# Tracing the transposed a and the products N V inside the second half of a chunk inverse, in a two-layer RWKV-7 and differential-attention encoder

## The chip, the cores and the metric

The kernel runs on one core of one Trainium2 chip. The metric is the device time of one execution in microseconds (us). Three executions of the kernel before were timed; the median counts.

## The reference, cut to what matters

The model has two layers over 2048 rows of width 1024. Layer 0 is RWKV-7 time mixing in parallel with a small cross-attention; layer 1 is differential attention. Only layer 0 bears on this change. Per head it runs this recurrence over time:

```python
z = z + (token_shift(z) - z) * mu
r, k, v, wd, ad = split(z)
kk = k * k_k;  kk = kk * rsqrt(max(sum(kk * kk), 1e-12))
def step(state, inp):
    sa = einsum('bhvk,bhk->bhv', state, -kk_t)
    state = state * w_t + sa[..., None] * (kk_t * a_t) + v_t[..., None] * k_t
    y_t = einsum('bhvk,bhk->bhv', state, r_t)
    return state, y_t
```

z is the normalised input times a wide weight; the output y is normalised per head and gated before the output projection.

## The kernel before, in words

The kernel computes the recurrence in chunks of 64 rows. Inside a chunk the rank-one updates are a triangular system, so each chunk needs the inverse of a 64x64 unit triangular matrix and a few products with it; between chunks a 64x64 state per head is carried.

Layer 0 goes over two halves of 1024 rows; in each half over six pairs of heads; in each pair over two blocks of 512 rows. One pair and block is a `Step`, 24 in all. A step handles 8 chunks of two heads at once. Its parts are methods of `Step`, and the loop at the end of `layer_a` traces them in this order for i = 0, 1, ...: `p2` and `p3` of step i+1, `p4b` and `p5` of step i, `p3b` and `p4` of step i+1, then `filler(i + 2)`, which traces the gate of step i+1 and `p1` of step i+2.

- `p1` makes the projections. Each (`pj`, line 174) is 24 products of 128x512 that accumulate in one bank of PSUM: the gate `sil`, then `kx`, `rx` and `vx`. Line 295 (ACT) and lines 296 to 298 (DVE) mix a projection with its shifted self. From `kx` follow `kk` (line 357, DVE), its square `rn` (line 359, ACT) and the product `pss` (line 367, TensorE), which sums the squares. `cum` and `Pt` (lines 344 to 355) are the decays, from the small products `lr`.
- `p2` makes the products `pg` and their masked copy `Gm`, and the transposes `bkp` and `pvt`.
- `p3` inverts 16x16 diagonal blocks by 15 levels of two small DVE operations (`itmp` and `Ti`, lines 453 and 455) and writes them out in two layouts, `T16` (lines 460 and 462) and `TT16` (lines 464 and 466).
- `p3b` puts the blocks together to `TT`: two rounds of products `inv` (line 481, with the copy `E1` between them), then `Ta` (line 487), the products `invz`, their copy (line 496), the products `invr`, and the copy into `TT` (line 502).
- `p4` makes the transposed a (`atp`, line 520, 8 products against the identity) and N V (`nvp`, line 528, 16 products), copies both, negated, into the two tiles `X` (lines 522 and 530, ACT), multiplies by the inverse (`txp`, line 539), copies the results to `Wn` and `UV`, and makes `mrp` and the first part of `ch` (line 563).
- `p4b` carries the state through 8 chunks: for each a product `ch` (line 574) and a scaled copy to `S` on ACT (line 575), which the next `ch` reads; and the outputs `yp` (lines 583 and 588).
- `p5` copies them to `ys` (line 590), takes statistics (line 597), subtracts and scales (lines 607 and 608), transposes (`py`, line 611) and stores.

The order on each engine isn't written out by hand. The order in which the code is traced gives each instruction its priority; a scheduler then places instructions of neighbouring steps between each other on every engine at build time. On the chip each engine runs its list. Small tiles of `p3` to `p4` share the tag "iv" of 4 buffers (`M_`, `E1`, `X1`, `X2`, `T16`, `TT16`, `X`, `Wn`), and small PSUM tiles share the tag "gm" of 3 banks.

Of the kernel before, what the change touches and what calls it, by code (L numbers as in the profile page):

```python
# [10 lines left out]
AF = mybir.ActivationFunctionType  # L11
# [4 lines left out]
P = 128  # L16
# [8 lines left out]
C = 64  # L25
TB = 512
NC = TB // C
NJ = NC // 2
# [31 lines left out]
def hybrid_kernel(ctx, tc, S, HALF, x, mem, pv, cv, dist, postn, w_out, w_mkv, a_w, w2, a2, w_kv, b_w, out):  # L60
# [3 lines left out]
    mm = nc.tensor.matmul  # L64
    V = nc.vector
    A = nc.scalar
# [18 lines left out]
    def cc(name, w):  # L85
        return cvt[:, CV[name]:CV[name] + w]

    ident = cc("ident", 128)
# [120 lines left out]
    def layer_a(ph):  # L209
# [31 lines left out]
        def T(shape, name, bufs=1, tag=None, dt=F32):  # L241
            return pa.tile(shape, dt, name=name, tag=tag or name, bufs=bufs)
# [7 lines left out]
        def I(shape, name, dt=F32):  # L250
            return pa.tile(shape, dt, name=name, tag="iv", bufs=4)

        def PS(shape, name, tag="gm", bufs=3):
            if tag == "pj":
                return ppj.tile(shape, F32, name=name, tag="pj", bufs=3)
            return pps.tile(shape, F32, name=name, tag=tag, bufs=bufs)
# [69 lines left out]
        class Step:  # L326
# [141 lines left out]
                self.t3 = Nv, E1, T16, TT16  # L468

            def p3b(self):  # L470
                Nv, E1, T16, TT16 = self.t3

                TT = T([P, NJ, 2, 64], "TT", 1)

                def blk16(lt, rt_):
                    pb = PS([P, NJ, 2, 64], "inv")
                    for j in range(NJ):
                        for hh in range(2):
                            for q in range(2):
                                rows = slice(q * 64, q * 64 + 64)  # L480
                                mm(pb[rows, j, hh, :], lhsT=lt[rows, j, hh, :], rhs=rt_[rows, j, hh, :], start=True, stop=True)
                    return pb
                A.activation(E1, blk16(E1, T16), AF.Copy)
                V.tensor_tensor(out=TT, in0=blk16(E1, TT16), in1=TT16, op=ALU.add)

                Ta = T([P, NJ, 2, 32], "Ta", 1)
                V.transpose(out=Ta.rearrange("p j h t -> p (j h) t"), in_=TT.rearrange("p j h t -> p (j h) t")[:, :, 0:32])
                pz = PS([P, NJ, 2, 32], "invz")
                pr = PS([P, NJ, 2, 32], "invr")
                qa, qb = ([slice(q * 64 + o, q * 64 + o + 32) for q in range(2)] for o in (0, 32))  # L490
                for j in range(NJ):
                    for hh in range(2):
                        for q in range(2):
                            mm(pz[qb[q], j, hh, :], lhsT=Nv[q][0:32, j, hh, 32:64], rhs=Ta[qa[q], j, hh, :], start=True, stop=True)
                for q in range(2):
                    A.activation(Ta[qb[q]], pz[qb[q]], AF.Copy)
                for j in range(NJ):
                    for hh in range(2):
                        for q in range(2):
                            mm(pr[qa[q], j, hh, :], lhsT=Ta[qb[q], j, hh, :], rhs=TT[qb[q], j, hh, 32:64], start=True, stop=True)  # L500
                for q in range(2):
                    V.tensor_copy(out=TT[qa[q], :, :, 32:64], in_=pr[qa[q]])
                self.TT = TT
# [4 lines left out]
            def p4(self):  # L508


                AR, Gm, BKT, UV, TT = self.AR, self.Gm, self.BKT, self.UV, self.TT
                ar = (slice(64, 128), slice(0, 64))
                rr = (slice(0, 64), slice(64, 128))
                hcs = (slice(0, 64), slice(64, 128))

                X = [I([P, 2, 2, P], "X") for g in range(2)]
                pt = PS([P, NJ, P], "atp")
                for j in range(NJ):
                    for e in range(2):
                        mm(pt[ar[e], j, :], lhsT=AR[:, 2 * j + e, ar[e]], rhs=ident, start=True, stop=True)  # L520
                for g in range(2):
                    A.activation(X[g][:, :, :, 0:C], pt.rearrange("p j (h k) -> p j h k", h=2)[:, g * 2:g * 2 + 2], AF.Copy, scale=-1.0)
                pn = PS([P, NJ, 2, C], "nvp")
                for j in range(NJ):
                    for hh in range(2):
                        for e in range(2):
                            c = 2 * j + e
                            mm(pn[ar[e], j, hh, :], lhsT=Gm[rr[e], e, j, hh, ar[e]], rhs=UV[rr[e], c, hcs[hh]], start=True, stop=True)
                for g in range(2):
                    A.activation(X[g][:, :, :, C:P], pn[:, g * 2:g * 2 + 2], AF.Copy, scale=-1.0)  # L530
                Wn = I([P, NJ, 2, C], "Wn")
                UV4 = UV.rearrange("p (j e) (h v) -> p j e h v", e=2, h=2)
                for g in range(2):
                    js = slice(g * 2, g * 2 + 2)
                    px = PS([P, 2, 2, P], "txp")
                    for j in (g * 2, g * 2 + 1):
                        for hh in range(2):
                            for e in range(2):
                                mm(px[ar[e], j % 2, hh, :], lhsT=TT[ar[e], j, hh, :], rhs=X[g][ar[e], j % 2, hh, :], start=True, stop=True)
                    A.activation(Wn[:, js], px[:, :, :, 0:C], AF.Copy)  # L540
                    for e in range(2):
                        A.activation(UV4[ar[e], js, e], px[ar[e], :, :, C:P], AF.Copy)

                MT = self.MTs
                MT4 = MT.rearrange("p (j e) k -> p j e k", e=2)
                RT = T([P, NC, C], "RT", 1)
                AR4 = AR.rearrange("p (j e) t -> p j e t", e=2)
                pmr = [PS([P, NJ, P], "mrp") for e in range(2)]
                for j in range(NJ):
                    for hh in range(2):  # L550
                        for e in range(2):
                            mm(pmr[e][hcs[hh], j, 0:C], lhsT=Wn[ar[e], j, hh, :], rhs=BKT[ar[e], 2 * j + e, hcs[hh]], start=True, stop=True)
                            mm(pmr[e][hcs[hh], j, C:P], lhsT=Wn[ar[e], j, hh, :], rhs=Gm[ar[e], e, j, hh, rr[e]], start=True, stop=True)
                for e in range(2):
                    for hh in range(2):
                        hs = hcs[hh]
                        V.tensor_tensor(out=MT4[hs, :, e, hs], in0=pmr[e][hs, :, 0:C], in1=ident[hs, None, hs].broadcast_to([C, NJ, C]), op=ALU.add)
                    V.tensor_tensor(out=RT.rearrange("p (j e) t -> p j e t", e=2)[:, :, e], in0=pmr[e][:, :, C:P], in1=AR4[:, :, e, rr[e]], op=ALU.add)

                ch = pps.tile([P, NC, C], F32, name="ch", tag="ch", bufs=2)  # L560
                for c in range(NC):
                    for hh in range(2):
                        mm(ch[hcs[hh], c, :], lhsT=BKT[:, c, hcs[hh]], rhs=UV[:, c, hcs[hh]], start=c == 0, stop=False, skip_group_check=True)
                self.MT, self.RT, self.ch = MT, RT, ch
# [228 lines left out]
    class MemAttn:  # L793
# [30 lines left out]
        def T(self, shape, name, dt=F32, bufs=None):  # L824
            return self.pool.tile(shape, dt, name=name, tag=name, bufs=bufs or 1)

        def tile(self, t, yh, yl, PS):
# [7 lines left out]
            for m in range(2):  # L835
# [4 lines left out]
                mx = T([P, 4], "mmx")  # L840
                V.tensor_reduce(out=mx[:, 0:2], in_=ps, op=ALU.max, axis=AX.X)  # L841
                V.tensor_scalar(out=mx[:, 0:2], in0=mx[:, 0:2], scalar1=-SCALE, scalar2=None, op0=ALU.mult)
# [290 lines left out]
    def layer_b_attn(ep, prefetch):  # L1133
        with ExitStack() as st:
# [38 lines left out]
            def scores(u):  # L1173
# [3 lines left out]
                for qt in range(2):  # L1177
# [7 lines left out]
                    for c in range(2):  # L1185
# [16 lines left out]
                        E.append(e)  # L1202
                    V.tensor_reduce(out=nm[:, 0:2], in_=mx[:, :, 0:nkb], op=ALU.min, axis=AX.X)  # L1203
                    for c in range(2):
# [77 lines left out]
    with pool_(name="w_next", bufs=1) as rp:  # L1282
# [17 lines left out]
        for i in range(KT):  # L1300
            hf, k = i // 4, slice(i % 4 * 2, i % 4 * 2 + 2)
# [81 lines left out]
```

## Time and profile before

| | |
|---|---|
| median of three runs | 3139.35 us (3136.95 to 3140.87) |
| the profiled execution's own time | 3131.17 us |
| its span, first to last instruction | 3129.4 us |
| TensorE (PE) busy in the span | 2944.0 us, 94% |
| VectorE (DVE) / ScalarE (ACT) / GpSimd (POOL) busy | 57% / 48% / 27% |
| layer 0 | up to about 1420 us of the span |

PE, PEld, DVE, ACT, POOL are the engines (PEld is the load of TensorE's stationary operand). A matmul of 4-byte numbers can stand as two records in the trace, so record counts there can be twice those of the program. "PEclk" is TensorE's granted clock as a share of full speed: 1.00 is 2.4 GHz, 0.50 is 1.2 GHz.

### The profile page before, as it was taken

What the parts mean: (1) busy time and instruction counts of PE and PEld (TensorE: products, weight loads), DVE (VectorE), ACT (ScalarE), POOL (GpSimd) and SP (SyncE); (2) the same over time, 40 slices, a digit from 0 to 9 for tenths busy, and PEclk for the clock granted to TensorE, in tenths of its full rate; (3) what the DMA queues carried; (4) which work ended last, traced back from release to release, by engine and by line L of the source; (5) the groups of instructions that cost most, each with busy time, mean ns of one, the idle gap of its engine ahead of it and who ended that gap; (6) DMA issues with size and microseconds to landing.
All of it is one profiled execution on the core that took longest, in us unless ns stands there. A gap on an engine that the chain in (4) does not pass through costs nothing. (4 is left out here: it accounts for less than half of the span.)

```text
span 3129.4 us, 57336 instructions
## 1 busy us (share of the span) xinstructions
PE 2944.0 (94%) x22378; PEld 2390.8 (76%) x22378; DVE 1794.5 (57%) x4728; ACT 1504.3 (48%) x3310; POOL 840.2 (27%) x881
## 2 busy tenths in 40 slices
PE   6889999997899999998999999999999999998999
PEld 4767777776677777777777798888887888786777
DVE  6566767655676767673565311101118988887554
ACT  5545454545545454444454513213226777776443
POOL 3143423432243433431001212302212222323000
PEclk8899999998899999999999999999999999999999
DMA  3211000122011000115544533433355455543453
GB/s 119 78 33 37 28 24 23 39 61 84 26 30 37 28 24 24 38 45 142 147 135 127 147 86 91 118 86 92 102 164 123 101 113 115 122 85 103 129 153 116
DMA packets 262895, 264.13 MB, mean 84 GB/s; under 512 B 16736, under 2 KB 203232, under 8 KB 262496
## 3 DMA queue, kind: packets, MB, share of 16 engines
q1 hardware_dynamic: 234464, 193.87, 21.4%
q0 software_dynamic: 28160, 66.60, 10.4%
q8 instruction: 176, 2.88, 0.4%
q14 instruction: 95, 0.78, 0.1%
HBM read 179.14 MB, written 81.26 MB: 83 GB/s over the span
## 5 line engine op out<-in xcount | busy, mean ns | idle before, releaser
L174 PE MATMUL pj<-hhi,wh 128*128 128x512 f32 x928 | 389.6, 420 | 9.2 <-ACT sil L301 2.6
L174 PE MATMUL pj<-hhi,wl 128*128 128x512 f32 x928 | 375.3, 404 | 0.6 <-POOL wl L123 0.6
L174 PE MATMUL pj<-hlo,wh 128*128 128x512 f32 x928 | 368.5, 397 | 0.0
L123 POOL TENSOR_TENSOR wl<-wraw,wh 128x512 fp32r<-128x512 f32 x160 | 210.5, 1325 | 497.2 <-ACT wh L122 477.3
L1200 DVE CUSTOM_DVE_ANT_0 E<-s,dist 128x512 f32<-128x512 f32 (+1 forms) x480 | 276.1, 605 | 35.0 <-PE s L1198 28.9
L174 PE MATMUL pj<-bh,wh 128*128 128x512 f32 x672 | 262.8, 391 | 0.0
L174 PE MATMUL pj<-bh,wl 128*128 128x512 f32 x672 | 262.6, 391 | 0.0
L174 PE MATMUL pj<-bl,wh 128*128 128x512 f32 x672 | 262.5, 391 | 0.0
L1205 ACT ACTIVATE E<-E,nm 128x1920 f32<-128x1920 f32 (+7 forms) x192 | 229.4, 1199 | 59.1 <-DVE nm L1203 58.6
L174 PEld LDWEIGHTS pj<-hhi,wh 128*128 128x128 f32 x928 | 175.8, 189 | 63.7 <-ACT sil L301 8.9
L1238 PE MATMUL o<-th,vs 128*128 128x256 f32 (+1 forms) x864 | 211.0, 376 | 2.3 <-ACT th L1231 0.9
L1197 PE MATMUL s<-ks,qd 128*128 128x512 f32 (+1 forms) x480 | 205.6, 432 | 2.2 <-DVE mx L1200 1.2
L174 PEld LDWEIGHTS pj<-hhi,wl 128*128 128x128 f32 x928 | 175.4, 189 | 40.7 <-POOL wl L123 1.5
L174 PEld LDWEIGHTS pj<-hlo,wh 128*128 128x128 f32 x928 | 176.2, 190 | 38.8 <-issue 5.5
L122 ACT ACTIVATE wh<-wraw 128x512 fp32r<-128x512 f32 x160 | 100.3, 627 | 217.0 <-PE pj L174 139.4
L1238 PEld LDWEIGHTS o<-th,vs 128*128 128x128 f32 x864 | 153.9, 189 | 38.3 <-ACT th L1231 18.8
L1198 PE MATMUL s<-ks,qd 128*128 128x512 f32 (+1 forms) x480 | 176.1, 373 | 0.0
L174 PEld LDWEIGHTS pj<-bh,wh 128*128 128x128 f32 x672 | 126.7, 189 | 26.4 <-DVE ot L936 0.3
L174 PEld LDWEIGHTS pj<-bh,wl 128*128 128x128 f32 x672 | 126.6, 188 | 26.3
L174 PEld LDWEIGHTS pj<-bl,wh 128*128 128x128 f32 x672 | 126.6, 188 | 26.1
L1231 ACT ACTIVATE th<-tr 128x512 f32<-128x512 f32 (+1 forms) x216 | 113.2, 568 | 44.1 <-PE tr L1228 43.7
L1208 DVE SCALAR_TENSOR_TENSOR E<-E,nm,E 128x1920 f32<-128x1920 f32 (+7 forms) x96 | 132.1, 1376 | 0.9
(421 smaller groups left out, 6983.8 us busy)
## 6 DMA issues: line engine op xcount, KB each, us to landing
wraw<-in_a_w SPq DMA_DIRECT2D x118, 256.0 KB, 2.9
qd<-qd_d POOLq DMA_DIRECT2D x48, 512.0 KB, 7.0
mq<-mq POOLq DMA_DIRECT2D x64, 256.0 KB, 4.6
yr<-y_dram SPq DMA_DIRECT2D x32, 384.0 KB, 5.0
ks<-ks_d POOLq DMA_DIRECT2D x24, 512.0 KB, 7.0
xt<-in_x SPq DMA_DIRECT2D x16, 512.0 KB, 5.5
x_dram<-ot SPq DMA_DIRECT2D x16, 512.0 KB, 4.3
wraw<-in_b_w SPq DMA_DIRECT2D x32, 256.0 KB, 3.0
```

The lines of the kernel that those rows point to most:

```text
L122: A.activation(hi[:, ks], raw, AF.Copy)
L123: eng.tensor_tensor(out=lo[:, ks], in0=raw, in1=hi[:, ks].bitcast(F32), op=ALU.subtract)
L174: mm(ps, lhsT=w[a_][:, k, wcol], rhs=h[b_][:, k, tsl], start=n == 0, stop=n == 3 * KT - 1)
L1197: mm(ps[:, f:f + w_], lhsT=qd[:, 0, c, qs], rhs=k_[:, c, 0:w_], start=True, stop=False)
L1198: mm(ps[:, f:f + w_], lhsT=qd[:, 1, c, qs], rhs=k_[:, c, 0:w_], start=False, stop=True)
L1200: V.tensor_tensor_reduce(out=e[:, kb * 512:kb * 512 + w], in0=ps[:, 0:w], in1=dt_[:, u0:u0 + w], scale=-SLOPES[h], scalar=3.0e38, op0=ALU. ...
L1205: A.activation(E[c][:, 0:nk], E[c][:, 0:nk], AF.Exp, bias=nm[:, c:c + 1], scale=-1.0, accum_out=nm[:, 2 + c:3 + c])
L1208: V.scalar_tensor_tensor(out=E[0][:, 0:nk], in0=E[1][:, 0:nk], scalar=nm[:, 5:6], in1=E[0][:, 0:nk], op0=ALU.mult, op1=ALU.add)
L1231: A.activation(th[:, 0:w], ps[:, 0:w], AF.Copy)
L1238: mm(po[:, oc], lhsT=vs[kt // 4][:, kt % 4, :], rhs=th[:, rc], start=n == 0, stop=n >= nmm - 2, skip_group_check=True)
```

## The change

The tiles `X`, the 8 products `atp`, the 16 products `nvp` and the four ACT copies into `X` are traced in `p3b`, after the second `inv` product and the sum `TT`, and before `Ta`. Until now they stood at the head of `p4`, after the end of the inverse. The operations, their shapes and their inputs stay what they were.

```diff
@@ p3b
             def p3b(self):
+                Gm = self.Gm
                 Nv, E1, T16, TT16 = self.t3
...
                 A.activation(E1, blk16(E1, T16), AF.Copy)
                 V.tensor_tensor(out=TT, in0=blk16(E1, TT16), in1=TT16, op=ALU.add)
+                AR, UV = self.AR, self.UV
+                ar = (slice(64, 128), slice(0, 64))
+                rr = (slice(0, 64), slice(64, 128))
+                hcs = (slice(0, 64), slice(64, 128))
+
+                X = [I([P, 2, 2, P], "X") for g in range(2)]
+                pt = PS([P, NJ, P], "atp")
+                for j in range(NJ):
+                    for e in range(2):
+                        mm(pt[ar[e], j, :], lhsT=AR[:, 2 * j + e, ar[e]], rhs=ident, start=True, stop=True)
+                for g in range(2):
+                    A.activation(X[g][:, :, :, 0:C], pt.rearrange("p j (h k) -> p j h k", h=2)[:, g * 2:g * 2 + 2], AF.Copy, scale=-1.0)
+                pn = PS([P, NJ, 2, C], "nvp")
+                for j in range(NJ):
+                    for hh in range(2):
+                        for e in range(2):
+                            c = 2 * j + e
+                            mm(pn[ar[e], j, hh, :], lhsT=Gm[rr[e], e, j, hh, ar[e]], rhs=UV[rr[e], c, hcs[hh]], start=True, stop=True)
+                for g in range(2):
+                    A.activation(X[g][:, :, :, C:P], pn[:, g * 2:g * 2 + 2], AF.Copy, scale=-1.0)
+                self.X = X
 
                 Ta = T([P, NJ, 2, 32], "Ta", 1)
@@ p4: the same lines are removed here
-                X = [I([P, 2, 2, P], "X") for g in range(2)]
...
+                X = self.X
                 Wn = I([P, NJ, 2, C], "Wn")
```

Since the scheduler places everything anew, the lists of three engines change around it. The excerpts below show a steady step of the first half; in them lines after the insertion have other numbers than before (+1 and +22 inside `p3b`, +7 from `txp` on).

TensorE, from the end of `p4` (`ch`, 16 products on UV) to `pss` of the next `p1`; `pj` here is the projection of kx ahead of `pss` and that of rx behind it. Before:

```order
L563 MATMUL ch<-UV,BKT 64x64 x16
L367 MATMUL pss<-rn,cvt 128x512
L174 MATMUL pj<-hhi,wh 128x512
L174 MATMUL pj<-hlo,wh 128x512
L174 MATMUL pj<-hhi,wl 128x512
```

and after the change:

```order
L570 MATMUL ch<-UV,BKT 64x64 x16
L174 MATMUL pj<-hhi,wh 128x512
L174 MATMUL pj<-hlo,wh 128x512
L174 MATMUL pj<-hhi,wl 128x512
L174 MATMUL pj<-hhi,wh 128x512
L174 MATMUL pj<-hlo,wh 128x512
L174 MATMUL pj<-hhi,wl 128x512
L581 MATMUL ch<-sb_124,MT 128x64
L581 MATMUL ch<-S,MT 128x64 x2
L367 MATMUL pss<-rn,cvt 128x512
```

The last six products of the projection of kx now stand directly ahead, and after them the first three of the eight state products, which were in `p4b` behind `pvt`. This holds in 19 steps; in one more, two of the three are there.

ACT, from the copies of `txp` and `invz` to the square `rn` and its two successors (`wh` is a weight being rounded; it stands here in every second step). Before:

```order
L496 ACTIVATE Ta<-invz 32x256 x2
L295 ACTIVATE kx<-pj,omu 128x512
L354 ACTIVATE Pt<-cum 128x520
L122 ACTIVATE wh<-wraw 128x512
L522 ACTIVATE X<-atp 128x4x64 x2
L355 ACTIVATE cum<-cum 128x520
L530 ACTIVATE X<-nvp 128x4x64 x2
L359 ACTIVATE rn<-kk 128x512
L540 ACTIVATE Wn<-txp 128x256
L542 ACTIVATE UV<-txp 64x2x128 x2
```

and after the change:

```order
L549 ACTIVATE UV<-txp 64x2x128 x2
L122 ACTIVATE wh<-wraw 128x512
L295 ACTIVATE kx<-pj,omu 128x512
L354 ACTIVATE Pt<-cum 128x520
L582 ACTIVATE S<-ch,PC 128x64
L355 ACTIVATE cum<-cum 128x520
L582 ACTIVATE S<-ch,PC 128x64
L122 ACTIVATE wh<-wraw 128x512
L359 ACTIVATE rn<-kk 128x512
L582 ACTIVATE S<-ch,PC 128x64
L369 ACTIVATE rn<-rn 128x512
```

The X copies have gone up the list, ahead of the copies of `invz`; the copy of kx now stands behind all copies of `txp`, and the first two state copies stand between it and the square `rn`.

DVE, from the end of the statistics of `p5` to the two layouts of the inverse's blocks (`sm`: statistics; `ys`: the outputs; `Ti`, `itmp`: the 15 levels). Before:

```order
L460 TENSOR_SCALAR X_5816<-Ti,cvt 128x16x16 x2
L601 TENSOR_TENSOR sm<-bs 128x8
L602 SCALAR_TENSOR_TENSOR sm<-sm 128x8
L462 STREAM_TRANSPOSE T_5819<-X_5816 128x16x32
L464 TENSOR_SCALAR X_5815<-Ti,cvt 128x16x16 x2
L603 TENSOR_TENSOR sm<-sm 128x8
L604 TENSOR_SCALAR sm<-sm 128x8
L466 STREAM_TRANSPOSE TT_5823<-X_5815 128x16x32
L607 TENSOR_TENSOR ys<-ys,sm 128x512
L304 TENSOR_SCALAR e_sil<-e_sil 128x512
L345 TENSOR_SCALAR cum<-cum 128x8x64
L608 TENSOR_TENSOR ys<-ys,sm 128x512
```

and after the change:

```order
L610 TENSOR_TENSOR sm<-sm 128x8
L611 TENSOR_SCALAR sm<-sm 128x8
L453 TENSOR_TENSOR itmp<-Dd,Ti 128x39
L614 TENSOR_TENSOR ys<-ys,sm 128x512
L455 TENSOR_TENSOR Ti<-Ti,itmp 128x3x13
L615 TENSOR_TENSOR ys<-ys,sm 128x512
L453 TENSOR_TENSOR itmp<-Dd,Ti 128x28
L455 TENSOR_TENSOR Ti<-Ti,itmp 128x2x14
L453 TENSOR_TENSOR itmp<-Dd,Ti 128x15
L455 TENSOR_TENSOR Ti<-Ti,itmp 128x15
L460 TENSOR_SCALAR X_5816<-Ti,cvt 128x16x16 x2
L462 STREAM_TRANSPOSE T_5819<-X_5816 128x16x32
```

The scaling of `ys`, on which `py` waits, now comes ahead of the end of the 15 levels and of both layouts; before it came behind them.

## Rows read from the trace of the kernel before

**Rows 1.** The page, part 1: busy time and share of the span, instructions.
```profile
PE 2944.0 (94%) x22378; PEld 2390.8 (76%) x22378; DVE 1794.5 (57%) x4728; ACT 1504.3 (48%) x3310; POOL 840.2 (27%) x881
```

**Rows 2.** Windows, two steps each: length, busy us of each engine, PEclk, DMA share.
```profile
949.57:1049.90 100.33, 94.02 (x1072) 75.14 (x1073) 69.77 (x187) 47.94 (x106) 38.12 (x35) 1.00 0.10 29
1049.90:1150.36 100.46, 94.01 (x1072) 75.14 (x1073) 69.73 (x187) 47.96 (x106) 38.10 (x35) 1.00 0.10 29
```

**Rows 3.** Waits of PE in these four steps: us in total, times, longest us.
```profile
PE py L611 <- DVE ys L608: 4.2, 4, 1.2
PE txp L539 <- ACT X L530: 1.9, 4, 0.5
...
PE invz L494 <- DVE Ta L487: 0.7, 2, 0.3
PE pj L174 <- ACT sil L301: 0.5, 2, 0.3
```

**Rows 4.** Timeline of PE in one step: start us, us, line, names, shapes, [idle before].
```profile
1006.75 0.40 PE L174 MATMUL pj<-hlo,wh 128*128 128x512 f32 x1
1006.99 0.39 PE L174 MATMUL pj<-hhi,wl 128*128 128x512 f32 x1
...
1010.63 1.75 PE L539 MATMUL txp<-X,TT 64*64 64x128 f32 x28 [0.48 <-ACT X L530]
...
1014.17 1.15 PE L563 MATMUL ch<-UV,BKT 128*64 128x64 f32 x32
1015.26 1.12 PE L367 MATMUL pss<-rn,cvt 128*128 128x512 f32 x2
...
1034.88 0.43 PE L574 MATMUL ch<-S,MT 128*128 128x64 f32 x2 [0.16 <-ACT S L575]
...
1036.08 0.33 PE L574 MATMUL ch<-S,MT 128*128 128x64 f32 x2
1036.34 0.33 PE L588 MATMUL yp<-S,RT 64*64 64x64 f32 x4
```

**Rows 5.** Timeline of ACT in the same step.
```profile
1007.42 0.69 ACT L295 ACTIVATE kx<-pj,omu 128x512 f32<-128x512 f32 x1
1008.00 0.63 ACT L354 ACTIVATE Pt<-cum 128x520 f32<-128x520 f32 x1
1008.66 0.64 ACT L355 ACTIVATE cum<-cum 128x520 f32<-128x520 f32 x1
1009.21 0.64 ACT L522 ACTIVATE X<-atp 128x256 f32<-128x256 f32 x2
...
1035.36 0.31 ACT L575 ACTIVATE S<-ch,PC 128x64 f32<-128x64 f32 x1 [0.53 <-PE ch L574]
```

**Rows 6.** Groups of ACT in the four steps of rows 2: count, busy, mean ns.
```profile
L122 ACT ACTIVATE wh<-wraw 128x512 fp32r<-128x512 f32 x16 | 10.0, 626 | 24.6 <-PE pj L174 15.2 <-DMA wraw<-in_a_w 9.4
...
L359 ACT ACTIVATE rn<-kk 128x512 f32<-128x512 f32 x4 | 2.5, 632 | 0.7 <-DVE kk L357 0.7
```

**Rows 7.** Timeline of DVE in the same step.
```profile
1008.14 0.75 DVE L296 SCALAR_TENSOR_TENSOR kx<-pj,pvt,kx 128x511 f32<-128x511 f32 x1 [2.49 <-ACT kx L295]
...
1010.08 0.48 DVE L357 TENSOR_SCALAR kk<-kx,pvt 128x512 f32<-128x512 f32 x1
...
1041.95 0.23 DVE L597 BATCH_NORM_STATS2 bs<-ys 128x6 f32<-128x64 f32 x1 [0.29 <-ACT ys L590]
...
1044.81 1.08 DVE L462 STREAM_TRANSPOSE T<-X 128x512 f32<-128x512 f32 x1
...
1048.52 1.24 DVE L608 TENSOR_TENSOR ys<-ys,sm 128x512 f32<-128x512 f32 x1
```

**Rows 8.** Windows around long waits of PE in layer 0; columns as rows 2.
```profile
838.00:842.00 4.00, 0.26 (x2) 0.00 (x0) 3.77 (x13) 2.92 (x5) 0.28 (x2) 0.95 0.17 66
873.00:877.00 4.00, 1.56 (x7) 0.94 (x5) 2.84 (x4) 1.73 (x3) 3.02 (x2) 1.00 0.18 55
1280.00:1285.00 5.00, 4.21 (x18) 3.27 (x19) 4.75 (x9) 1.47 (x3) 3.45 (x3) 0.69 0.38 108
```

More of the change, by code (lines that the diff above doesn't have):

```diff
@@ L514, in p4 @@
                 hcs = (slice(0, 64), slice(64, 128))
-                X = [I([P, 2, 2, P], "X") for g in range(2)]
[L517 to L530, printed above, removed]
+                X = self.X
                 Wn = I([P, NJ, 2, C], "Wn")
```

## The prediction

> **What bounds the kernel now.** I read the page's busy shares first: PE is busy for 94% of the span, no other engine for more than 57% [rows 1]. So layer 0 can only become shorter or longer where PE waits, or where its work changes; the change adds and removes no operation. Then two windows of two steps each: 100.33 and 100.46 us, so a steady step takes 50.2 us, and the clock is at 1.00, which is 2.4 GHz [rows 2]. The waits of PE in these four steps show what can be won: `py` on DVE's `ys` 4.2 us, `txp` on the X copies 1.9, `invz` on `Ta` 0.7, a projection on `sil` 0.5 [rows 3]. Per step that is 1.05, 0.48, 0.17 and 0.13 us, 1.83 in all. The waits of PE on other things (`pg`, `mrp`) lie outside the moved piece and I leave them as they are. Last I read one step as a timeline on PE, ACT and DVE [rows 4, 5, 7], to see how long the round trips between engines are that the new order puts next to each other.
>
> **The change, part by part.**
>
> *The moved products cover a wait.* `atp` and `nvp`, 24 products, now run on PE between the second `inv` and `invz`. There they cover the sum `TT` and the transpose `Ta`, and the projection products that used to do so now stand ahead of `txp`, where they cover the X copies and the copy into `TT`. I cost the waits of `txp` and `invz` at nothing from now on: 0.65 us a step won. The 0.13 of `sil` goes too, since `py` and part of `lr` now come before the next projection. Sum: −0.78 us.
>
> *`py` comes earlier, and so does what it waits for.* In a steady step three of the eight `ch` and six projection products have left the stretch ahead of `py`, and 22 wide products instead of 28 or 32 stand between the last `yp` and `py`. On DVE, `ys` is now scaled ahead of both layouts: the transposes of 1.08 us each and the four scalings around them no longer stand before line 608, which began 6.57 us after the first statistics and took 1.24 [rows 7]. Laying both lists out by the durations of one step, PE arrives at `py` some 4.3 to 5.2 us earlier and DVE is done some 5.6 us earlier. The wait of 1.05 falls to about 0.3; its ends are 0 and 1.05. I take −0.75.
>
> *Two small new waits.* The first `inv` needs `T16`, whose layout DVE now makes after `ys`: four small operations, two scalings and the transpose of 1.08 us [rows 7] come after line 608, about 2.4 us, while PE has `py` and six wide products, about 2.1. I take 0.25, ends 0 and 0.6. `invr` needs the copy of `invz`, which on ACT now stands behind the four X copies and behind the exponentials that start only after `TT16`; by ACT's durations it comes between 0.1 and 0.45 us late. I take 0.25, ends 0 and 0.6. Sum: +0.5.
>
> *The price: the way from kx to `pss` loses its cover.* Before, the last product of kx began at 1006.99 and `pss` at 1015.26; in the 8.3 us between, PE ran `invr`, `atp`, `nvp`, `txp`, `mrp` and `ch` [rows 4]. Now only three `ch` stand there. What `pss` needs takes longer than these. Count from the start t of that last product. ACT's copy of kx starts at t+0.43, `Pt` 0.58 later, at t+1.01 [rows 4, 5]. The first `ch` starts at once, but its copy S stands behind `Pt` on ACT, so it starts at about t+1.6 and takes 0.31; the second `ch` starts at t+1.95 instead of t+0.5. The second S needs that `ch` (a copy starts 0.48 after its product, 1034.88 to 1035.36) and stands behind `cum`, 0.64 us: it ends at t+2.85, and the third `ch` starts at t+2.9 [rows 4, 5]. `rn` stands behind the second S and needs `kk`; DVE starts its part 0.72 after the kx copy [rows 5, 7], and four operations with the last of 0.48 us end by t+2.75. So `rn`, 0.63 us [rows 6], ends at t+3.5, and `pss` starts at t+3.6. PE worked 3 x 0.26 us of `ch` in it, from t+0.23 on (a `ch` of rows 4 holds PE 0.26, as 1036.08 to 1036.34 shows). It waits for 3.6 − 0.23 − 0.78 = 2.6 us; with the first `ch` a little later, as after a change of tile shape, 2.4. I take 2.5. In every second step a `wh` of 0.63 us [rows 6] stands between the second S and `rn`: 0.55 more, 0.27 on average. Sum: +2.77. All three engines run these lists as written, so nothing else can fill the hole; the rx and vx products stand behind `pss`.
>
> The state products that moved up shorten `p4b`, but there they had cost almost no wait: one of 0.16 in every second step [rows 4]. Nothing is won there, apart from `py`, counted above. No DMA and nothing of SP's or POOL's is moved by hand; POOL's few operations keep their order and have gaps.
>
> *Sum.* A steady step: −0.78 − 0.75 + 0.5 + 2.77 = +1.74 us. It holds for 20 of 24 steps, +35 us. The other four (the first, the last and two at the turn of the halves) win `txp` and `invz`, 4 x 0.65 = 2.6, so −3. Together +32 us on the profiled execution, 3131.17 + 32 = 3163 us. That execution lies 8 us under the median of the runs shown, 3139.35; the difference carries over, which gives **3171 us**. Ends: with no wait left or new at `py`, `inv` and `invr` and no `wh` in the way, a step gets 2.5 − 1.83 = +0.67, in all +10, 3150 us. With `py` as before, 0.6 at both small ones and a `wh` in every step it gets 3.05 + 1.2 − 0.78 = +3.47, in all +66, 3206 us.
>
> **The rivals.**
>
> *Faster.* The X copies are what `txp` waits for, and they now start some microseconds sooner; if the wait ahead of `pss` doesn't come, a step wins 1.53 us, and the kernel 20 x 1.53 + 2.6 = 33 us: 3106 us. It decides at a wait of about 1.0 us a step ahead of `pss`: below it the change wins. For it speak the waits of rows 3, which do go. Against it speaks that copy, mix and square alone are 0.69 + 0.75 + 0.48 + 0.63 = 2.55 us one after the other [rows 5, 6, 7] against 0.78 us of work. Chance 0.05. The Trainium skill, "Perfetto Trace Analysis", section "Identifying Performance Opportunities", tells one to find the gaps of the most contended engine and make what they wait for start sooner; that is this change, and by it alone the time would be this one. The rule says nothing of what the moved work had covered.
>
> *No change.* The wait ahead of `pss` comes out near 1 us, because kx's products finish earlier in the list than I count, and the two sums cancel to within 6 us, 3139 us. The list shows six kx products directly ahead of `ch`, which speaks against it. Chance 0.05.
>
> *Slower, by the clock too.* Around 838 to 842 PE was busy for 0.26 of 4 us, and the clock fell to its lower level, 1.2 GHz; at 873 to 877 it was busy for 1.56 of 4 and the clock stayed at 1.00; at 1280 to 1285 it fell, to 0.69 on average, though PE was busy for 4.21 of 5 [rows 8]. The new hole, 0.78 us of work in 3.4, looks most like the second case. If the clock falls in each step as in the third, a step loses 0.31 x 5 = 1.55 us more, 31 in all: 3202 us. Chance 0.08. The Trainium skill, "TensorE: Matmul & The Clock Gate", section "HAM oscillation", describes kernels in which a wait in every pass brings the clock down every time; by that rule this rival would be the likeliest, and the second case of rows 8 is why I don't take it so.
>
> That the change doesn't do what it says is no rival: the lists show `atp` and `nvp` moved.
>
> **How the numbers follow.** The forecast, slower by the sum above, gets 0.82, the clock 0.08, no change 0.05, faster 0.05. 0.2%, about 6 us, is what a measurement of this kernel can tell from no change. Hence faster 0.05, the same 0.05, slower 0.90. The range is that of the bounds, 3150 to 3206 us; it takes in the clock's 3202 and leaves out the other two rivals and somewhat of either tail.
>
> **What would show it.** In the profile after, the waits of PE should have `txp` on X and `invz` on `Ta` gone, and as new and largest ones `ch` on S with about 2 us a step and `pss` on `rn` with 0.4 to 0.9; `py` near 0.3. A pair of steps should take about 104 us instead of 100.4, with the hole between the projection of kx and `pss`, and ACT busy through it with kx, `Pt`, S, `cum`, S, `rn`. PE's busy time should stay within some us of 2944, unless the clock falls. The forecast is wrong if a pair takes 100 us or less, or if `ch` and `pss` together wait less than 1 us a step; the step at fault is then the order of the copies on ACT. If PE's windows behind `pss` show less than 1.00 in most steps, the clock is the mis-sized part.

## The result and the profile after

PE is the matrix engine, DVE, ACT, POOL the vector, scalar and GpSimd engines, as in the profile; the expectations write TensorE, VectorE and ScalarE for the first three.

| | before | after |
|---|---|---|
| median of 4 runs, us | 3138.94 (3136.95 to 3140.87) | 3219.34 (3202.76 to 3240.17) |
| profiled execution, us | 3131.17 | 3240.17 (the longest of the four) |
| its span, us | 3129.4 | 3238.2 |
| PE busy, us | 2944.0 | 2995.9 |
| mean granted clock of PE | 0.979 | 0.958 |

The changed kernel takes 1.0259 of the time before (95% interval 1.0228 to 1.029), 80 us more. Slower was forecast, 32 us of it; 3219 lies above the range of 3150 to 3206.

The page, part 1, answers to [rows 1]:

```profile
PE 2995.9 (93%) x22378; PEld 2425.1 (75%) x22378; DVE 1813.9 (56%) x4728; ACT 1502.0 (46%) x3310; POOL 831.4 (26%) x881
```

The same 22378 records of products take 52 us more. Two steady steps, from `pss` to `pss`, in the columns of [rows 2]:

```profile
1081.50:1194.10 112.60, 100.24 (x1073) 79.07 (x1073) 72.32 (x186) 47.70 (x106) 36.97 (x35) 0.92 0.09 26
```

The same two steps before (1115.7 to 1216.1, also `pss` to `pss`) took 100.40 us, 94.06 of them busy. So a pair lost 12.2 us: 6.2 where PE is busy, at a clock of 0.92 instead of 1.00, and 6.0 where it waits. The pairs at the ends of a half of layer 0 lose less: over the ten pairs it is 105 us of the 109 by which the two profiled executions differ.

This is the longest of the four runs, and the one with the lowest clock. The other three took 3216.77, 3221.90 and 3202.76 us at mean clocks of 0.966, 0.963 and 0.969, so over the four a clock lower by 0.001 goes with some 3.3 us. By that the low clock costs some 20 us less in the median run than here, and of the median's 80 us some 30 to 40 are the clock's; the rest is waits. This is an estimate: 30 is what is left of the 52 us, and 39 us came back with the clock in run 1 below.

The waits of PE in this pair (us, times, longest) answer to [rows 3], which hold two pairs:

```profile
PE ch L581 <- ACT S L582: 3.9, 5, 1.6
PE pg L406 <- DVE carry L298: 2.3, 2, 1.7
PE inv L482 <- DVE T L462: 2.2, 2, 1.6
PE invz L516 <- DVE Ta L509: 2.0, 1, 2.0
...
PE pss L367 <- ACT rn L359: 0.7, 3, 0.3
PE py L618 <- DVE ys L615: 0.4, 1, 0.4
```

`txp` on X and the projection on `sil` are gone, `py` is small, `ch` on S with `pss` is the largest: as forecast. `inv`, `invz` and `pg` were not forecast at this size. The hole ahead of `pss`, timeline of PE (start, us, line, names, [idle before]), answers to [rows 4]:

```profile
1130.58 0.39 PE L174 MATMUL pj<-hhi,wl 128*128 128x512 f32 x1
1130.81 0.33 PE L581 MATMUL ch<-sb,MT 128*128 128x64 f32 x2
1132.77 0.43 PE L581 MATMUL ch<-S,MT 128*128 128x64 f32 x2 [1.63 <-ACT S L582]
1133.61 0.69 PE L581 MATMUL ch<-S,MT 128*128 128x64 f32 x2 [0.40 <-ACT S L582]
1134.65 2.08 PE L367 MATMUL pss<-rn,cvt 128*128 128x512 f32 x2 [0.35 <-ACT rn L359]
```

ACT over the same 4 us, which answers to [rows 5]:

```profile
1131.32 0.67 ACT L295 ACTIVATE kx<-pj,omu 128x512 f32<-128x512 f32 x1
1131.89 0.63 ACT L354 ACTIVATE Pt<-cum 128x520 f32<-128x520 f32 x1
1132.41 0.30 ACT L582 ACTIVATE S<-ch,PC 128x64 f32<-128x64 f32 x1
1132.61 0.63 ACT L355 ACTIVATE cum<-cum 128x520 f32<-128x520 f32 x1
1133.24 0.31 ACT L582 ACTIVATE S<-ch,PC 128x64 f32<-128x64 f32 x1
1133.45 0.62 ACT L122 ACTIVATE wh<-wraw 128x512 fp32r<-128x512 f32 x1
1133.97 0.62 ACT L359 ACTIVATE rn<-kk 128x512 f32<-128x512 f32 x1
```

This is the order that was worked out: kx, `Pt`, S, `cum`, S, `wh`, `rn`, with PE waiting for each S and for `rn`. The last product of kx begins at 1130.58, `pss` at 1134.65, 4.07 us later (4.15 was worked out for a step with `wh`). In the steps without `wh` it is 3.33 us for 3.6.

What was not expected stands in the windows behind the waits; the last column but two is the granted clock, as in [rows 8]:

```profile
1082.00:1086.00 4.00, 4.00 (x11) 2.81 (x10) 0.69 (x1) 1.26 (x2) 0.93 (x1) 0.57 0.00 0
1133.00:1141.00 8.00, 7.25 (x19) 4.97 (x19) 2.70 (x5) 3.06 (x7) 3.33 (x3) 0.57 0.22 66
1153.00:1158.00 5.00, 5.00 (x24) 3.94 (x24) 4.29 (x7) 1.20 (x2) 2.62 (x3) 0.66 0.26 74
1181.00:1185.00 4.00, 4.00 (x42) 2.63 (x42) 0.83 (x2) 0.21 (x1) 0.00 (x0) 0.57 0.01 2
```

In each, PE works nearly all the time, and at 1.2 GHz for most of it. They come behind the hole of one step (1082), late in that of the next and behind it (1133), behind a wait of `pg` (1153) and behind the wait of `invz` (1181). From one pair to the next this repeats in this run. Before, the windows of the steady steps show such a stretch at three places in all (near 280, 380 and 1281).

### The profile page after: what moved, and what is told of

It reads as the page before. It is cut to its first block, busy times and chain, and to the rows that moved or that the text cites. A ratio compares the mean times of both kernels' runs of the same rounds, so it can differ in the third digit from the quotient of the medians.

```text
span 3238.2 us, 57334 instructions
## 1 busy us (share of the span) xinstructions
PE 2995.9 (93%) x22378; PEld 2425.1 (75%) x22378; DVE 1813.9 (56%) x4728; ACT 1502.0 (46%) x3310; POOL 831.4 (26%) x881
## 5 line engine op out<-in xcount | busy, mean ns | idle before, releaser
L174 PE MATMUL pj<-hhi,wh 128*128 128x512 f32 x928 | 409.3, 441 | 7.6 <-DVE hlo L149 1.8
L174 PE MATMUL pj<-hlo,wh 128*128 128x512 f32 x928 | 384.6, 414 | 0.0
L174 PEld LDWEIGHTS pj<-hhi,wh 128*128 128x128 f32 x928 | 184.9, 199 | 63.2 <-issue 8.4
L174 PEld LDWEIGHTS pj<-hlo,wh 128*128 128x128 f32 x928 | 185.4, 200 | 46.9 <-issue 10.3
L174 PEld LDWEIGHTS pj<-hhi,wl 128*128 128x128 f32 x928 | 184.5, 199 | 41.5 <-POOL wl L123 1.5
```

Of the source, the lines that this page charges most:

```text
L174: mm(ps, lhsT=w[a_][:, k, wcol], rhs=h[b_][:, k, tsl], start=n == 0, stop=n == 3 * KT - 1)
```

## The experiments

Three theories stood at the start. A: the hole ahead of `pss` costs its waits and sets off the low clock. B: the clock falls because of the waits for `T16`, `Ta` and the `pg` tiles. C: the clock is lower whatever the order. An "edge" in the edits orders two instructions of one engine; the scheduler then places all others anew around it.

**1. Fill the hole with useless work.** The order is pinned by edges of this kind to what it is in the changed kernel, and ten products go into the waits ahead of `pss`.

```diff
                 pss = PS([P, TB], "pss", "pj")
+                self.fill = [[mm(pss, lhsT=lora[:, 0], rhs=th[0], start=True, stop=True) for _ in range(g)] for g in ((6, 2, 2) if p else (0, 0, 0))]
...
+                            for d_ in nxt.fill[c]:
+                                behind(d_, m_)
+                            if c == 2:
+                                behind(nxt.pss_i, m_)
```

`m_` is the state product c, `behind` adds the edge.

> The changed kernel with its order of work unchanged, and ten useless products of 128x512 a step (0.21 us each at 2.4 GHz, 2.1 us a step) that fill the waits ahead of pss in the 20 steady steps: six behind the first state product, two behind the second, two behind the third. Their result is overwritten by pss. They save no wait: what TensorE waited (about 2.15 us a step) it now works. Theory A (the hole ahead of pss sets off the low clock behind it, about 10 us at 1.2 GHz in two steps): the falls right behind pss go, those behind pg (1153) and invz (1179) stay, and the kernel with more work is faster: about 50 us under 3219, 3160 to 3180. Theory B (the falls come from the waits for T16, Ta and the pg tiles, and the hole only costs itself): no gain, 3210 to 3235. Theory C (the clock is lower in this kernel whatever its order): 3210 to 3235 too, with falls behind pss as before.

Measured: 3180.67 us, 1.0134 of before (1.0118 to 1.0151), 39 us under the changed kernel with 200 products more. Timeline of PE in a filled hole, of a step with `wh`:

```profile
1096.73 0.33 PE L594 MATMUL ch<-sb,MT 128*128 128x64 f32 x2
1096.87 1.64 PE L375 MATMUL pss<-th,lora 128*128 128x512 f32 x6
...
1100.33 1.02 PE L376 MATMUL pss<-rn,cvt 128*128 128x512 f32 x2
```

Two steps, from this hole to the next but one:

```profile
1096.90:1202.50 105.60, 98.28 (x1095) 78.10 (x1094) 71.09 (x186) 47.87 (x106) 37.52 (x35) 0.98 0.09 28
```

`pss` comes 3.60 us after the first `ch`, against 3.84 at 1130.81 of the changed kernel: the useless products delay nothing. The clock in the pair is 0.98 instead of the 0.92 of the longest run. The waits for `T16` (1.56) and `Ta` (1.95) are still there. B and C fall; A is right in kind and 1 us outside its numbers. One low stretch is left in this pair, behind `invz` (1142); the one behind `pg`, which A had staying, is gone too, and `pg` waits 1.0 us at most instead of 1.7. So part of the loss is the low clock that goes with the hole: 39 us came back although PE has 200 products more to do.

**2. Take away the wait for `Ta`.** VectorE's scan goes behind the transpose.

```diff
+                scan = V.tensor_tensor_scan(cumf, cc("smask", NC * 65), cumf, 0.0, op0=ALU.mult, op1=ALU.add)
+                if self.ta is not None:
+                    tc.add_manual_dep(scan.ins, self.ta.ins.name, mybir.DependencyInfo(mybir.DependencyClass.NoSync, mybir.DependencyReason.DATA), reason="order")
```

> The changed kernel, in which VectorE's scan of cum comes behind the transpose of Ta in the ten steps where it stood ahead of it; TensorE's order is untouched. Theory A: only the wait of invz (1.97 us in ten steps) goes, and with it the fall of 3 us at 1.2 GHz behind it (1.5 us): 20 plus 15, so 3180 to 3195; the holes ahead of pss and their falls stay. Theory B (these waits carry the loss): more than half of the 80 us comes back, under 3175. Theory C: the 20 us of the wait alone, about 3200.

Measured: 3200.71 us, 1.0204 (1.0189 to 1.0219). `invz` waits no more for `Ta`, 16 us in all, and 19 us came back; the mean clock, 0.967, is within that of the changed kernel's four runs (0.958 to 0.969). So the wait cost itself; these clocks don't show whether the low clock got less without it. A was 6 us too low, B is missed, and the number is the one of C, which run 1 had ruled out. The 19 us is a difference of two medians, one of them of runs that lie 37 us apart.

**3. Put the state products back behind `pss`.**

```diff
+                    m_ = mm(ch[:, c, :], lhsT=MT[:, c, :], rhs=st[c], start=False, stop=True, skip_group_check=True)
+                    if c == 0 and after is not None:
+                        tc.add_manual_dep(m_.ins, after.ins.name, mybir.DependencyInfo(mybir.DependencyClass.NoSync, mybir.DependencyReason.DATA), reason="order")
...
+            steps[i].p4b(steps[i + 1].pss_i if i + 1 < n else None)
```

> The changed kernel with one edge added: the first state product of a step is held behind pss of the next step, where it stood in the kernel before. All that the change moves inside the inverse stays moved. Theory A: the hole ahead of pss goes with its falls, T16 and Ta are waited for as in the changed kernel or somewhat longer; 2.15 us x 20 of waits and 50 us of clock come back: 3115 to 3150. Theory B: only the 2.15 us x 20 come back, the falls stay: 3170 to 3195. Theory C: the same as B, with the clock still at about 0.965.

Measured: 3168.94 us, 1.0104 (1.0089 to 1.0119). The clock is back (0.978), but not the time. In every second step two products of kx still stand behind the `ch` products, now with nothing between them and `pss`:

```profile
1034.76 0.50 PE L174 MATMUL pj<-hlo,wh 128*128 128x512 f32 x1
1035.10 0.40 PE L174 MATMUL pj<-hhi,wl 128*128 128x512 f32 x1
1038.43 1.21 PE L367 MATMUL pss<-rn,cvt 128*128 128x512 f32 x2 [2.94 <-ACT rn L359]
```

Ten such waits are 29 us. That is as much as the loss of 30, but only in sum: `txp` waits 10 us less than before, and PE is busy 2962.1 us, 18 longer. A failed: it took the state products for the cause. The time is 1 us under B's range, but B had the low clock stay.

**4. Fill the hole with useful work.** Half of the projection of r goes ahead of `pss`.

```diff
+                else:
+                    prx = PS([P, TB], "pj", "pj")
+                    proj(prx, ws[1], h, slice(0, TB), ks=range(0, 4))
...
-                    mix(pj(ws[1], h), p, rx)
+                    proj(prx, ws[1], h, slice(0, TB), ks=range(4, KT))
+                    mix(prx, p, rx)
```

> The changed kernel with the first twelve products of the projection of r (2.6 us at 2.4 GHz) written ahead of pss: its accumulator is then taken earlier and the products stand in the hole; the three state products go back behind pss as well. Theory A: no hole, no fall behind pss, 3110 to 3150. Theory B: only the holes' own 43 us come back: 3170 to 3195. Theory C: as B, clock about 0.965.

Measured: 3170.45 us, 1.0103 (1.0086 to 1.0119). The hole is gone, but the time is in B's range and not in A's: `pg` now waits for AR. Waits of PE in layer 0:

```profile
PE pg L410 <- DVE AR L394: 32.7, 19, 2.6
```

From runs 3 and 4 came theory D: the last product of kx starts a chain of set length, over `pss`, `rn`, BK and AR to `pg`, and what matters is when that product ends and how much of PE's work is left beside the chain. Its rival E: the moved groups cost by themselves.

**5. The change without its side effect.** The last product of kx is held ahead of `txp`. `atp` and `nvp` stay moved; the state products fall back behind `pss` by themselves.

```diff
+                last = proj(pk, ws[0], h, slice(0, TB))
+                if p and self.txp_i is not None:
+                    tc.add_manual_dep(self.txp_i.ins, last.ins.name, mybir.DependencyInfo(mybir.DependencyClass.NoSync, mybir.DependencyReason.DATA), reason="order")
```

> The changed kernel with one edge added: the first txp product of a step is held behind the last product of the projection of k of the next. The transposed a and N V stay within the second half of the inverse, as the change puts them; the projection of k ends where it ended before, ahead of txp, and the state products are back behind pss. Theory D (formed from the runs before this: from the last product of k over pss to BK, AR and pg is a chain of set length; what lies beside it on TensorE was shortened by the two groups that the change moves ahead of the end of k, and whichever gap is filled, the rest of the wait stands at the next link, with a low clock behind it where the gap is long): the chain starts as early as before but has the two groups (about 2.5 us) less beside it, txp's wait of 0.48 and the 0.26 for sil may go: 3125 to 3155. Rival E (the moved groups cost by themselves, by their copies on ScalarE and the later T16 and Ta): 3160 to 3175, as the two runs that filled or emptied the hole. Theory A alone: under 3125.

Measured: 3137.7 us, 1.0006 (0.9994 to 1.0017): no change. The move itself costs nothing, so E falls, and it brings nothing either, within 0.2%. The one edge brings back more than the place of kx: in DVE's list the scaling of `ys` stands behind the first layout again, `py` waits 22.3 us in layer 0 (24.0 before, 6.4 in the changed kernel) and `inv` 13.9 (13.9 and 33.1). So this run shows that the loss lies in what the scheduler does around the move; which part of it costs what is left to the runs below. Two steps, and two groups of PE in them (count, busy us, mean ns):

```profile
1166.20:1266.90 100.70, 95.14 (x1076) 75.64 (x1072) 69.03 (x187) 47.81 (x106) 38.07 (x35) 1.00 0.10 29
```

```profile
L566 PE MATMUL mrp<-BKT,Wn 64*64 64x64 f32 x64 | 3.2, 238 | 0.8 <-ACT UV L556 0.7
L567 PE MATMUL mrp<-Gm,Wn 64*64 64x64 f32 x64 | 2.9, 218 | 0.0
```

PE waits 5.6 us in a pair instead of 6.3 (`txp` on X is gone), but is busy 1.1 us longer at the same clock: `mrp` 6.1 against 5.6 before, `invr` 1.9 against 1.7. Why the same narrow products hold PE longer here was not tried.

**6. The loss without the change.** Run 4's edit, made on the kernel before.

```diff
+                else:
+                    prx = PS([P, TB], "pj", "pj")
+                    proj(prx, ws[1], h, slice(0, TB), ks=range(0, 4))
...
-                    mix(pj(ws[1], h), p, rx)
+                    proj(prx, ws[1], h, slice(0, TB), ks=range(4, KT))
+                    mix(prx, p, rx)
```

> The kernel before, with nothing moved but the first twelve products of the projection of r, written ahead of pss. It has no hole there, so nothing is filled; 2.6 us of work leave the stretch between pss and pg. Theory D: pg waits for AR and BK instead, as in the changed kernel with the same edit (48 us of waits of pg against 23 before): 25 us more, 3155 to 3175. Rival E: no cost without the moved groups, 3130 to 3145.

Measured: 3169.25 us, 1.0111 (1.0096 to 1.0126). Waits of PE in layer 0, and `pss` and `pg` of one step:

```profile
PE pg L410 <- DVE AR L394: 35.2, 19, 2.6
```

```profile
1036.81 1.02 PE L370 MATMUL pss<-rn,cvt 128*128 128x512 f32 x2
...
1047.21 1.80 PE L410 MATMUL pg<-AR,BK 64*128 64x128 f32 x22 [1.20 <-DVE AR L394]
```

The same loss as in run 4, at the same place, with nothing moved: D's number holds, E falls again. But D's picture of one chain of set length from kx on does not hold. From the start of kx's last product to `pss` it is 10.8 and 10.6 us in two steps here, against 8.3 and 8.8 in the kernel before, so kx was in time. From `pss` to `pg` it is 10.4 and 11.8 us here and 9.7 and 11.7 in run 4, with waits for AR, against 12.0 and 12.1 before. So there are two links, each with a least length of its own: kx to `pss`, which was too short of cover in the changed kernel, and `pss` to `pg`, which is too short here.

**7 and 8. One group alone.** In the first `nvp` with its copies goes back to `p4`, so that only `atp` is moved; in the second `atp` goes back. Against the changed kernel, the first lines of each block:

```diff
-                pn = PS([P, NJ, 2, C], "nvp")
...
+                pn = PS([P, NJ, 2, C], "nvp")
```

```diff
-                pt = PS([P, NJ, P], "atp")
...
+                pt = PS([P, NJ, P], "atp")
```

> The transposed a alone is moved into the second half of the inverse; N V stays behind it. The last five to nine products of k still come behind the ch products, with three state products between them and pss. Theory D: the hole and its falls are as in the changed kernel: 3190 to 3225, and pss is waited for as long. Rival E: the cost goes with what is moved, about half: 3165 to 3185.

> N V alone is moved into the second half of the inverse; the transposed a stays behind it. As with the other half: theory D 3190 to 3225, the hole as long; rival E about half of the cost, 3165 to 3185.

Measured: `atp` alone 3231.06 us, 1.0308 (1.0275 to 1.034), 6 us above D's range; `nvp` alone 3215.27 us, 1.026 (1.0242 to 1.0278), within it. E's 3165 to 3185 is missed by both. The wait at the hole, in layer 0 up to 1450 us, of the one and of the other:

```profile
PE ch L581 <- ACT S L582: 44.6, 56, 2.7
```

```profile
PE ch L581 <- ACT S L582: 46.3, 58, 2.7
```

Either half costs as much as both (44.1 us of that wait in the changed kernel, 46.1 in run 2, which has its order on PE). The cost does not go with the amount moved: either move makes the scheduler leave the last five to ten products of kx behind `ch`, with three state products as their only cover.

**9. The changed kernel with six products moved.** Run 5's edge, and one that keeps the state products ahead of `pss`. PE's order differs from the changed kernel's in the last six products of kx, which stand ahead of `txp` (and in how the narrow `mrp` interleave). On ACT and DVE the copy and the mix of kx follow them and stand ahead of the copies to `Wn` and `UV` and of MT.

```diff
+                    if c == 2 and nxt is not None:
+                        tc.add_manual_dep(nxt.pss_i.ins, m_.ins.name, mybir.DependencyInfo(mybir.DependencyClass.NoSync, mybir.DependencyReason.DATA), reason="order")
```

> The changed kernel's own order, with one thing moved: the six last products of the projection of k (1.3 us) stand ahead of txp instead of behind the ch products. The three state products stay ahead of pss, the two groups stay within the inverse. Theory D (the end of k starts the chain over pss to pg; its place decides): no hole ahead of pss beyond the round trips of the state copies (two of 0.4 us), so no falls behind it; the waits for T16 and Ta stay (20 and 12 us over the kernel before, and the falls behind Ta): 3150 to 3185. Rival F (the state products ahead of pss make the hole, wherever k ends): as the changed kernel, 3200 to 3235.

Measured: 3175.02 us, 1.0131 (1.0113 to 1.0148), 44 us under the changed kernel. Two steps, and the largest waits in them:

```profile
1093.80:1199.60 105.80, 96.23 (x1074) 76.64 (x1074) 71.58 (x186) 47.95 (x105) 37.76 (x35) 0.97 0.09 28
```

```profile
PE inv L487 <- DVE T L467: 2.2, 2, 1.6
PE invz L521 <- DVE Ta L514: 1.9, 1, 1.9
PE ch L588 <- DVE MT L571: 1.6, 2, 0.8
...
PE ch L588 <- ACT S L591: 1.4, 4, 0.4
```

D holds, F falls: with kx early the state products wait 3.0 us in a pair for MT and S, where the hole had 4.3, and the clock is 0.97 instead of the 0.92 of the longest run. The waits for `T16` and `Ta` stay, as they should. 1.3 us of products a step in another place, with the copies that follow them, are worth 44 us in all.

**10 and 11. kx earlier still.** The edge goes from the last product of kx to the first of `atp` (10) or of `invr` (11).

> The changed kernel with the last product of k held ahead of the transposed a: k now ends some 5 us earlier than in the kernel before, pss comes ahead of txp, and the moved groups cover part of the chain again. Theory D: pg waits less for what the chain feeds (23 us of waits in the kernel before, of which some 10 may go), while txp may wait for TT with nothing but one product ahead of it (0.5 to 1 us a step): 3115 to 3150, a little under the kernel before if the first is the larger. Rival G (with k early the order of VectorE bounds the step, not the chain): no gain, 3140 to 3165.

> The changed kernel with the last product of k held ahead of invr: k ends about where it ended in the kernel before, the state products are behind pss, and invr runs in one piece. Theory D: within 10 us of the kernel before, 3130 to 3150; txp may wait up to 1 us for TT in its 20 steps. Rival E (the moved groups cost by themselves): 3160 to 3175.

Measured: 3170.64 us, 1.0112 (1.0097 to 1.0127), and 3150.78 us, 1.0051 (1.0034 to 1.0068). The first lies above both of its ranges, the second 1 us above D's. Each has a new wait in layer 0, of `invr` in the first and `txp` in the second:

```profile
PE invr L529 <- ACT Ta L525: 18.6, 42, 0.9
```

```profile
PE txp L553 <- DVE TT L531: 29.6, 22, 1.8
```

In the kernel before, products of kx stand between `invz` and `invr`, and `atp` and `nvp` between `invr` and `txp`. `pg` waits as long as before (27 and 23 us against 23), so an earlier kx brings nothing at the end of the chain. In run 10 `pss` comes 17 to 19 us ahead of `pg`, and its clock is lower too (0.970 to 0.972). Theory D holds for a kx that ends later than before, not for an earlier one; G, which had no gain, is right in kind only. No version here beats the kernel before.

**12. Runs 9 and 2 together.**

> The run with k early and the state products still ahead of pss, and with the scan of cum behind the transpose of Ta in ten steps: both edits together, nothing else. Theory D (the rest of that run's loss of 39 us is its waits for Ta, T16 and the state copies): the 16 us of invz go, and the one fall in two steps behind it (1.7 us, ten times): 3140 to 3160. Rival: as on the changed kernel itself, where the same edit gave back its wait and nothing of the clock: 3157 to 3165. If neither, over 3170.

Measured: 3155.83 us, 1.0065 (1.0048 to 1.0081): in D's range and 1 us under the rival's, so the two are hardly told apart. Of run 9's 39 us 19 came back, of them 16 of `invz`. What is left is 20 us. The largest wait in layer 0, 13.9 before:

```profile
PE inv L489 <- DVE T L469: 34.7, 22, 6.5
```

That is 21 us more than before; `ch` waits 25 us more for MT and S, `py` and `txp` 17 and 9 less. These come to 20, as much as is left. That is a sum of waits; no run takes away the wait for `T16` by itself.

## Why the prediction was wrong

**Right: what the change does to the list.** The hole ahead of `pss` is where it was said to be, made of the steps that were named, in their order on ACT. It was costed at 2.77 us a step; in the two holes of a pair `ch` and `pss` wait 4.3, some 2.1 a step. Run 9 shows its cause: with kx's last six products elsewhere it shrinks to the waits for MT and S.

**Right: what is won.** `txp` on X and `sil` went as said. `py` went from 2.1 to 0.4 in a pair, 0.85 a step for the 0.75 taken. Run 5, where the move stands and `py` waits as before, shows that this was won by the new order around the move, not by the move.

**Wrong, the main step: the clock at nothing.** "The new hole, 0.78 us of work in 3.4, looks most like the second case" chose the one of the three stretches in [rows 8] whose clock had held, and gave the fall of the third a chance of 0.08. In the profiled run the clock fell behind both holes of a pair, and behind `pg` and `invz` too. PE's busy time rose by 52 us, where the forecast had it within some us of 2944. That rival was the mechanism. It had one fall of 1.55 us a step, 31 us in all: half of what this longest run lost (6.2 a pair, 3.1 a step), but about what the median run lost to it by the estimate above, 30 to 40. What took the median past the rival's 3202 as well were the waits below. A single long wait at the turn of the halves was no model for a wait that comes back every 50 us with others close to it. The Trainium skill, "TensorE: Matmul & The Clock Gate", section "HAM oscillation", tells of a clock that is lost anew in each pass, and its next section, "A second HAM failure mode: psum-queue depth-cycling", of short idle times between groups of products that bring the same. The trace of the longest run agrees with both in that the low stretches come again in each pair; no single wait in the pair shown is longer than 2.0 us. The prediction had the first rule in hand and set it aside on one row; the sign it named for this case, less than 1.00 behind `pss` in most steps, is the one that came.

**Wrong, smaller: two waits read from one step.** "`invz` at nothing": DVE's order was read in a step in which `Ta` comes ahead of the scan. In every second step it is the other way round. The first `inv` was given 0.25 and waits 1.1 on average, 1.55 in the steps that scale a `wh`. Timeline of DVE in such a step, and of POOL at the start of it:

```profile
1168.86 1.74 DVE L460 TENSOR_SCALAR X<-Ti,cvt 128x256 f32<-128x256 f32 x2
...
1177.38 1.83 DVE L352 TENSOR_TENSOR_SCAN cum<-cvt,cum 128x520 f32<-128x520 f32 x1 [0.88 <-ACT cum L347]
1179.14 0.41 DVE L509 STREAM_TRANSPOSE Ta<-TT 128x256 f32<-128x256 f32 x1
```

```profile
1168.73 1.30 POOL L123 TENSOR_TENSOR wl<-wraw,wh 128x512 fp32r<-128x512 f32 x1 [10.21 <-ACT wh L122]
```

The two scalings took 1.74 us beside POOL's `wl`; they take 0.73 in the step read of the kernel before, with POOL idle. The scan waits 0.88 for ACT and takes 1.83, and `Ta` stands behind both. `pg` waits 2.3 in a pair against 1.6 and was left as it was. Together these waits make the pair lose 6.0 us of waiting where 3.5 was forecast, in spite of the smaller hole. Over ten pairs that is some 25 us more than the sum had.

**The range.** Its upper end, 3206, was built from waits alone at full clock. The longer busy time, 52 us in the profiled run, lay outside every term of it.

## What to carry to other kernels

When work is moved earlier to cover one wait, look at what the scheduler then leaves for later: here six products on which `pss` waits, and it did not matter which of the two groups had pushed them back. Follow that chain to its far end before filling the gap: work pulled into it came out as a wait at the next link, with the change and without it. And where new waits come back in each pass of a loop, several in a step, price the low clock behind them too: here it cost as much as the waits in the longest run, 6.2 against 6.0 us in two steps, and by the estimate two fifths to a half of the loss in the median one.

## What was not expected of the hardware

Useless products made a kernel faster: 200 of them, in the holes, took 39 us off.

The same wait in the same place was followed by a low clock in four of ten steps. In run 3, `pss` waits 2.94 us behind the same products in ten steps; windows up to two of these waits' ends and behind them:

```profile
1034.00:1039.00 5.00, 2.06 (x35) 1.32 (x29) 4.33 (x12) 2.48 (x4) 0.00 (x0) 1.00 0.02 5
1039.00:1043.00 4.00, 4.00 (x11) 3.01 (x10) 0.69 (x1) 1.26 (x2) 1.21 (x1) 0.57 0.00 0
1139.00:1144.00 5.00, 2.06 (x35) 1.44 (x34) 4.49 (x12) 2.48 (x4) 0.00 (x0) 1.00 0.00 0
1144.00:1148.00 4.00, 4.00 (x18) 3.01 (x17) 0.69 (x1) 1.26 (x2) 1.14 (x1) 1.00 0.00 0
```

The first wait ended at 1038.43, the second at 1143.58; before both PE was busy for 2.06 of 5 us. One was followed by 0.57, the other by 1.00. The holes of the changed kernel do the same. In its profiled run the hole of the steps with `wh` (1.63, 0.40, then 0.34 to 0.60 us for `pss`) was followed by a low clock in all nine steps that have it; in run 2, with the same order on PE and the same waits of `ch`, in five of nine. Two of them, whose `pss` began at 1115.88 and 1220.86:

```profile
1116.00:1120.00 4.00, 4.00 (x16) 2.96 (x17) 0.69 (x1) 1.30 (x3) 1.51 (x2) 1.00 0.29 86
1221.00:1225.00 4.00, 4.00 (x8) 2.48 (x9) 0.69 (x1) 1.27 (x3) 0.63 (x1) 0.50 0.32 92
```

What decides between them no run here was made to show. The four times of the changed kernel, which lie 37 us apart, fit this: the higher the mean clock, the shorter the run.
